# Hybrid decoder layer, down projection: the fourth weight sum of a seven-product unit by an accumulating transfer in place of VectorE

## The chip, the cores and the metric

The kernel runs on one core of one Trainium2 chip. The metric is device time in microseconds; the kernel before takes 2109.56 us (median of three runs, 2108.89 to 2110.98).

## What is computed

One decoder layer over 512 tokens of 2048 features, all in float32: a norm, one input projection, gated linear attention and differential attention side by side, an output projection, and a gated feed-forward part with a causal convolution of width 3. The part that matters here is the last matrix product of it:

```python
def conv_ffn(h, w_ffn_in, conv_w, conv_b, w_ffn_out):
    up = h @ w_ffn_in                                  # 512 x 2048 by 2048 x 11264
    a, b = up[..., :D_FF], up[..., D_FF:]
    ...
    return (jax.nn.gelu(a, approximate=True) * b) @ w_ffn_out   # 512 x 5632 by 5632 x 2048
```

The product with `w_ffn_out` is the down projection. 5120 of its 5632 rows go through the units described next, the other 512 through plain products at the very end.

## The kernel before

**Granules.** A matrix product in float32 is made of three products in a rounded format: the weights and the activations are both split into a high part and a low part, and high by high, high by low and low by high are added in a PSUM bank. Weights come in granules of 128 x 1024 elements (512 KB). For each granule ScalarE copies the raw weights into the high part (L137), VectorE subtracts that from the raw weights to get the low part (L138), and TensorE runs 12 matmuls of 128 x 512 on it (L1348 to L1350; L1348 and L1350 need the high part only, L1349 needs the low part). High and low parts lie in a ring of three places (`ring`), with a spare pair (`xhi`, `xlo`) for some granules. Each engine takes its instructions in a fixed order.

**Units.** The big products are done in blocks of two by two with seven products in place of eight (the Strassen-Winograd scheme). One such unit is an object of class `Unit`. `a` is 4 in the units of the up projection and 2 in those of the down projection (`down_unit`, L1358). There are ten down units, `downs[0]` to `downs[9]`; I call them units 0 to 9. A unit has seven segments of two granules each. They run in the order x0, z0, y0, z1, x1, y1, y2, but the next unit's x0 comes ahead of this unit's y2. Segments x0, z0, y0 and y2 use one running sum of weight blocks, `t`, two tiles in the pool `rt`:

- x0 uses t = B11, loaded by SyncE
- z0 uses t + B12; B12 is added by an accumulating transfer, issued by GpSimd right after x0 has split t (method `more`, L1192 to L1195: `dma_start` with `accum_op=ALU.add`, which reads the block from HBM and adds it to what is in SBUF)
- y0 uses t + B22; B22 is loaded by itself into the pool `raw` and added by VectorE (L1211)
- y2 uses t + B21; B21 is loaded by itself into `raw`, since x1 needs it alone, and added by VectorE (L1229)

Segment z1 uses B22, x1 uses B21, and y1 uses B22 + B12, where B12 is added to B22's tiles by a second pair of accumulating transfers, issued after z1 has split B22. So a unit of the kernel before has two pairs of accumulating transfers, 512 KB each transfer: I call them the x0 pair (needed by z0) and the z1 pair (needed by y1).

**Order.** The work around the change is written in segment order (loop from L1504 on), and a scheduler of the framework places the instructions on each engine; it put each L1229 shortly after the split of its tile in y0, although the text has it after y1. Unit 0 and the first segment of unit 1 are different: they are written out by hand (`run_in_order`, `change_over`, with their own additions at L1412 and their own transfers at L1454).

Of the kernel before, what the change touches and what calls it, by code (L numbers as in the profile page):

```python
# [13 lines left out]
ALU = mybir.AluOpType  # L14
# [21 lines left out]
def hybrid_layer(ctx: ExitStack, tc: tile.TileContext, x, attn_pre_norm, w_in, w_alpha_up, b_alpha,  # L36
# [16 lines left out]
    tt = nc.vector.tensor_tensor  # L53
# [46 lines left out]
    def load(src, a, by=None):  # L100
        raw = wpool.tile([P, GR], F32, name="raw", tag="raw", bufs=4)
        (by or nc.sync).dma_start(out=raw.rearrange("p (a b) -> p a b", a=a), in_=src)
        return raw
# [592 lines left out]
    class InUnit:  # L696
# [21 lines left out]
        def more(self, raws, i, j):  # L718
            for g in range(2):
                nc.gpsimd.dma_start(out=raws[g].rearrange("p (a b) -> p a b", a=4),  # L720
                                    in_=self.block(i, j, g), accum_op=ALU.add)
# [42 lines left out]
        def y0(self):  # L764
            self.b22 = self.load(1, 1)
            for g in range(2):
                tt(self.t[g], self.t[g], self.b22[g], ALU.add)
            self.run("y0", "s2", self.t)
            self.more(self.t, 1, 0)
            self.u10 = block_tile("u10")  # L770
            act(self.u10, self.banks["y"], AF.Copy)
# [13 lines left out]
        def y1(self):  # L785
            self.run("y1", "s7", self.b22)
            tt(self.u11, self.u11, self.banks["y"], ALU.subtract)  # L787
            self.done(1, 1, self.u11)
# [380 lines left out]
    class Unit:  # L1169
# [19 lines left out]
                hl = granule(None, self.a, raws[g], spare=extra[0] and turn[0] % 4 == 0)  # L1189
                self.prods(self.banks[c], op, g, hl, first)  # L1190

        def more(self, raws, j):  # L1192
            for g in range(2):
                nc.gpsimd.dma_start(out=raws[g].rearrange("p (a b) -> p a b", a=self.a),  # L1194
                                    in_=self.block(0, j, g), accum_op=ALU.add)  # L1195

        def x0(self):
            self.t = [load_t(self.block(0, 0, g), self.a) for g in range(2)]
# [9 lines left out]
        def y0(self):  # L1208
            self.b22 = [load(self.block(1, 1, g), self.a) for g in range(2)]
            for g in range(2):  # L1210
                tt(self.t[g], self.t[g], self.b22[g], ALU.add)  # L1211
            self.run("y0", "s2", self.t)
            self.out("y0", self.bank_of("y0"))

        def z1(self):
# [9 lines left out]
        def y1(self):  # L1225
            self.run("y1", "s7", self.b22)
            self.out("y1", self.bank_of("y1"))
            for g in range(2):
                tt(self.t[g], self.t[g], self.b21[g], ALU.add)  # L1229

        def y2(self):
            self.run("y2", "a22", self.t)
# [424 lines left out]
```

## Time and profile before

| What | Before |
|---|---|
| median of the runs | 2109.56 us |
| the profiled execution's own time | 2109.1 us |
| its span, first to last instruction | 2107.4 us |
| granted TensorE clock, mean | 0.995 |
| TensorE busy | 2065.7 us (98%) |
| VectorE busy | 1532.4 us (73%) |
| ScalarE busy | 985.8 us (47%) |
| GpSimd busy | 286.6 us (14%) |
| first and last matmul of the down units (L1348) | 1651.4 and 2054.1 us from the span's start |

Times of single events are counted from the span's start. A timeline row gives start, duration, engine, line, operation, tiles, and in brackets how long the engine sat idle before it and which instruction or transfer ended that. A row of the windows view gives a stretch, its length, the busy time of each engine with its number of instructions, the granted clock, the mean busy share of the 16 DMA engines, and their rate in GB/s. TensorE's matmuls overlap each other by more than a third, so the distance of their starts says more than their durations.

### The profile page before, as it was taken

Reading aid. Unit: us, or ns where it says so; the run is one execution under the profiler, and the core shown is the slowest. Engines: PE = TensorE matmul, PEld = TensorE weight load, DVE = VectorE, ACT = ScalarE, POOL = GpSimd, SP = SyncE. Lnnn points to the kernel's source line nnn. Section 1 sums busy time; section 2 is a strip of 40 time slices with the busy share of each in tenths; the row PEclk is TensorE's granted clock in tenths of the full one; section 3 lists DMA queues with packets and bytes.
Section 4 is the critical chain, followed back from the end, with each engine's and each line's share of the span. In section 5 each row is a group of like instructions: output and inputs, shape, how many; then the busy total and the mean of one; then the engine's idle time right before and its main releaser. Section 6 shows DMA issues by size and latency. Waiting matters only on the chain.

```text
span 2107.4 us, 35508 instructions
## 1 busy us (share of the span) xinstructions
PE 2065.7 (98%) x14449; PEld 1904.8 (90%) x14449; DVE 1532.4 (73%) x1842; ACT 985.8 (47%) x1268; POOL 286.6 (14%) x306
## 2 busy tenths in 40 slices
PE   7999999999999999999999999999999999999997
PEld 6699999999888889899999999999999878887786
DVE  5966777666763255986787877878777878888877
ACT  4544444455563233454554444454454554444443
POOL 0212222222200000011111011110110110111100
PEclk9999999999999999999999999999999999999999
DMA  5388878888755344447667577577676876776763
GB/s 209 102 201 185 200 172 178 179 199 196 172 180 196 99 150 160 138 104 193 151 149 189 144 165 186 133 169 171 157 172 168 231 214 175 186 198 156 172 168 140
DMA packets 280696, 358.60 MB, mean 170 GB/s; under 512 B 14592, under 2 KB 221876, under 8 KB 278612
## 3 DMA queue, kind: packets, MB, share of 16 engines
q1 hardware_dynamic: 191380, 259.85, 36.7%
q0 software_dynamic: 84800, 94.38, 29.8%
q8 instruction: 113, 1.85, 0.4%
q10 hardware_dynamic: 4352, 2.10, 0.3%
q14 instruction: 51, 0.42, 0.1%
HBM read 311.72 MB, written 44.56 MB: 169 GB/s over the span
## 4 chain that ended last, share of the span: by engine, by line
issue 52%; PE 40%; POOL 4%; DMA 2%; DVE 1%; ACT 1%; POOLq 0%; SPq 0%; DVEq 0%; ACTq 0%
PE bank L192 3%; PE bank L193 3%; PE bank L191 3%; PE bank L742 3%; PE bank L744 3%; PE bank L746 3%; PE bank L743 3%; PE bank L747 3%; PE bank L748 3%; POOL rt L1194 2%; POOL raw L1194 2%; PE bank L522 1%; PE bank L1349 1%; PE bank L1350 1%; PE bank L1348 1%
## 5 line engine op out<-in xcount | busy, mean ns | idle before, releaser
L137 ACT ACTIVATE ring<-raw 128x1024 fp32r<-128x1024 f32 x315 | 333.3, 1060 | 518.7 <-PE bank L1247 123.6
L138 DVE TENSOR_TENSOR ring<-raw,ring 128x1024 fp32r<-128x1024 f32 x315 | 384.4, 1224 | 245.5 <-ACT ring L137 242.1
L1248 PE MATMUL bank<-ah,ring 128*128 128x256 f32 x1280 | 353.7, 276 | 0.1
L1246 PE MATMUL bank<-ah,ring 128*128 128x256 f32 x1280 | 353.5, 276 | 0.0
L1247 PE MATMUL bank<-al,ring 128*128 128x256 f32 x1280 | 353.5, 276 | 0.0
L137 ACT ACTIVATE ring<-rt 128x1024 fp32r<-128x1024 f32 x221 | 232.9, 1059 | 232.1 <-PE bank L1247 145.0
L138 DVE TENSOR_TENSOR ring<-rt,ring 128x1024 fp32r<-128x1024 f32 x221 | 269.3, 1222 | 91.9 <-ACT ring L137 90.0
L1248 PEld LDWEIGHTS bank<-ah,ring 128*128 128x128 f32 x1280 | 240.3, 188 | 0.3 <-DVE ring L138 0.3
L1246 PEld LDWEIGHTS bank<-ah,ring 128*128 128x128 f32 x1280 | 240.3, 188 | 0.1
L1247 PEld LDWEIGHTS bank<-al,ring 128*128 128x128 f32 x1280 | 240.3, 188 | 0.1
L1349 PE MATMUL bank<-ring,ah 128*128 128x512 f32 x424 | 166.3, 392 | 6.5 <-DVE ring L138 6.5
L1350 PE MATMUL bank<-ring,al 128*128 128x512 f32 x424 | 165.3, 390 | 0.0
L1348 PE MATMUL bank<-ring,ah 128*128 128x512 f32 x424 | 158.4, 391 | 0.4 <-ACT ring L137 0.4
L191 PE MATMUL bank<-ring,ah 128*128 128x512 f32 x280 | 110.1, 399 | 1.9 <-ACT ring L137 1.9
L192 PE MATMUL bank<-ring,ah 128*128 128x512 f32 x280 | 111.3, 399 | 0.0
L193 PE MATMUL bank<-ring,al 128*128 128x512 f32 x280 | 110.3, 396 | 0.0
L1194 POOL DMA_DIRECT2D raw<-in_w_ffn_in_dram x40 | 51.0, 1277 | 407.3 <-DVE ring L138 404.4
L1349 PEld LDWEIGHTS bank<-ring,ah 128*128 128x128 f32 x424 | 79.6, 188 | 26.6 <-DVE ring L138 10.4
L1348 PEld LDWEIGHTS bank<-ring,ah 128*128 128x128 f32 x424 | 79.5, 188 | 18.9 <-ACT ring L137 2.1
L1350 PEld LDWEIGHTS bank<-ring,al 128*128 128x128 f32 x424 | 79.6, 188 | 16.3
L1194 POOL DMA_DIRECT2D rt<-in_w_ffn_in_dram x40 | 50.9, 1274 | 319.2 <-DVE ring L138 243.1
L746 PE MATMUL bank<-ring,ah 128*128 128x256 f32 x320 | 92.4, 289 | 0.2 <-DVE u L787 0.2
(346 smaller groups left out, 5691.8 us busy)
## 6 DMA issues: line engine op xcount, KB each, us to landing
raw<-in_w_ffn_in_dram SPq DMA_DIRECT2D x96, 512.0 KB, 5.3
raw<-in_w_in_dram SPq DMA_DIRECT2D x56, 512.0 KB, 4.8
raw<-in_w_ffn_out_dram SPq DMA_DIRECT2D x48, 512.0 KB, 6.4
raw<-in_w_in_dram POOLq DMA_DIRECT2D x40, 512.0 KB, 7.1
rt<-in_w_ffn_in_dram SPq DMA_DIRECT2D x40, 512.0 KB, 5.6
rt<-in_w_ffn_in_dram POOLq DMA_DIRECT2D x40, 512.0 KB, 6.1
raw<-in_w_ffn_in_dram POOLq DMA_DIRECT2D x40, 512.0 KB, 7.5
raw<-in_w_o_dram SPq DMA_DIRECT2D x32, 512.0 KB, 4.2
```

The lines of the kernel that those rows point to most:

```text
L137: act(hi, raw, AF.Copy)
L138: tt(lo, raw, hi.bitcast(F32), ALU.subtract)
L191: mm(banks[t], ah[:, t, s, :], w[0][:, k, :], start=st, stop=False)
L192: mm(banks[t], ah[:, t, s, :], w[1][:, k, :], start=False, stop=False)
L193: mm(banks[t], al[:, t, s, :], w[0][:, k, :], start=False, stop=sp)
L1194: nc.gpsimd.dma_start(out=raws[g].rearrange("p (a b) -> p a b", a=self.a), in_=self.block(0, j, g), accum_op=ALU.add)
L1246: mm(o, wh, sh[:, :, kk, :], start=start and kk == 0 and n == 0, stop=False, **NOW)
L1247: mm(o, wh, sl[:, :, kk, :], start=False, stop=False, **NOW)
L1248: mm(o, wl, sh[:, :, kk, :], start=False, stop=kk == HK - 1, **NOW)
L1348: mm(b[j], sh[:, o:o + P], w[0][:, q, :], start=start and st == 0, stop=False, **NOW)
L1349: mm(b[j], sh[:, o:o + P], w[1][:, q, :], start=False, stop=False, **NOW)
L1350: mm(b[j], sl[:, o:o + P], w[0][:, q, :], start=False, stop=st == 3, **NOW)
```

## The change

In down units 1 to 9 VectorE no longer adds B21 to t. In its place, right after y0 has split t, GpSimd issues a pair of accumulating transfers that read B21 from HBM once more and add it to the two tiles of t. I call this the y0 pair. The up projection's units (a == 4) and unit 0 keep VectorE's addition. B21 is still loaded by itself for x1.

```diff
-        def more(self, raws, j):
+        def more(self, raws, j, i=0):
             for g in range(2):
                 nc.gpsimd.dma_start(out=raws[g].rearrange("p (a b) -> p a b", a=self.a),
-                                    in_=self.block(0, j, g), accum_op=ALU.add)
+                                    in_=self.block(i, j, g), accum_op=ALU.add)
...
             self.run("y0", "s2", self.t)
+            if self.a == 2:
+                self.more(self.t, 0, 1)
             self.out("y0", self.bank_of("y0"))
...
         def y1(self):
             self.run("y1", "s7", self.b22)
             self.out("y1", self.bank_of("y1"))
-            for g in range(2):
-                tt(self.t[g], self.t[g], self.b21[g], ALU.add)
+            if self.a == 4:
+                for g in range(2):
+                    tt(self.t[g], self.t[g], self.b21[g], ALU.add)
```

Lines after L1212 have numbers higher by two or three in the changed kernel: L1349 is L1352, L1356 is L1359.

VectorE, from y0 to x1 of unit 4, before. The rows with `rt` at L138 are y0's two splits, those with `raw` are z1's two and the first of x1; L1356 adds a PSUM bank to the output sums, L151 splits activations:

```order
L138 TENSOR_TENSOR ring<-rt,ring 128x1024
L1356 TENSOR_TENSOR acc_16862<-acc_16862,bank 128x512
L1356 TENSOR_TENSOR acc_16863<-acc_16863,bank 128x512
L1229 TENSOR_TENSOR rt<-rt,raw 128x1024
L151 TENSOR_TENSOR al<-st,ah 128x1024
L138 TENSOR_TENSOR ring<-rt,ring 128x1024
L138 TENSOR_TENSOR ring<-raw,ring 128x1024
L1356 TENSOR_TENSOR acc_16862<-acc_16862,bank 128x512
L1229 TENSOR_TENSOR rt<-rt,raw 128x1024
L1356 TENSOR_TENSOR acc_16863<-acc_16863,bank 128x512
L138 TENSOR_TENSOR xlo<-raw,xhi 128x1024
L138 TENSOR_TENSOR ring<-raw,ring 128x1024
```

VectorE at the same place in the changed kernel:

```order
L138 TENSOR_TENSOR ring<-rt,ring 128x1024
L1359 TENSOR_TENSOR acc_16862<-acc_16862,bank 128x512
L1359 TENSOR_TENSOR acc_16863<-acc_16863,bank 128x512
L151 TENSOR_TENSOR al<-st,ah 128x1024
L138 TENSOR_TENSOR ring<-rt,ring 128x1024
L138 TENSOR_TENSOR ring<-raw,ring 128x1024
L1359 TENSOR_TENSOR acc_16862<-acc_16862,bank 128x512
L1359 TENSOR_TENSOR acc_16863<-acc_16863,bank 128x512
L138 TENSOR_TENSOR xlo<-raw,xhi 128x1024
L138 TENSOR_TENSOR ring<-raw,ring 128x1024
```

The two additions are gone, and the rest stands in the same sequence, so y0's second split moves up by one place and z1's second by two.

GpSimd's transfers in the down units, before, from unit 3's z1 pair to unit 5's x0 pair. The names carry buffer numbers: `rt_17950` and `rt_17952` are unit 4's t, `raw_18058` and `raw_18060` its B22:

```order
L1194 DMA raw_17806<-in_w_ffn_out_dram 128x2x512
L1194 DMA raw_17808<-in_w_ffn_out_dram 128x2x512
L1194 DMA rt_17950<-in_w_ffn_out_dram 128x2x512
L1194 DMA rt_17952<-in_w_ffn_out_dram 128x2x512
L1194 DMA raw_18058<-in_w_ffn_out_dram 128x2x512
L1194 DMA raw_18060<-in_w_ffn_out_dram 128x2x512
L1194 DMA rt_18206<-in_w_ffn_out_dram 128x2x512
L1194 DMA rt_18208<-in_w_ffn_out_dram 128x2x512
```

GpSimd's transfers at the same place in the changed kernel, up to unit 5's x0 pair:

```order
L1194 DMA raw_17806<-in_w_ffn_out_dram 128x2x512
L1194 DMA raw_17808<-in_w_ffn_out_dram 128x2x512
L1194 DMA rt_17950<-in_w_ffn_out_dram 128x2x512
L1194 DMA rt_17952<-in_w_ffn_out_dram 128x2x512
L1194 DMA rt_17950<-in_w_ffn_out_dram 128x2x512
L1194 DMA rt_17952<-in_w_ffn_out_dram 128x2x512
L1194 DMA raw_18058<-in_w_ffn_out_dram 128x2x512
L1194 DMA raw_18060<-in_w_ffn_out_dram 128x2x512
L1194 DMA rt_18206<-in_w_ffn_out_dram 128x2x512
L1194 DMA rt_18208<-in_w_ffn_out_dram 128x2x512
```

The y0 pair (the second pair on `rt_17950` and `rt_17952`) stands between unit 4's x0 pair and its z1 pair, so the z1 pair is now behind it on GpSimd and on its queue.

On TensorE the scheduler also changes something: in the kernel before there are 33 places where it put two to four high-part products (L1348) of a granule ahead of the first low-part product (L1349); in the changed kernel there are 15, and elsewhere high, low and third product follow each other matmul by matmul. SyncE's order differs in one place only (two loads swapped in the last 50 us), ScalarE's in one (two neighbours swapped).

## The prediction

> **What bounds the kernel now.** I read the page first, then cut out the stage of the change, then asked there what TensorE waits for.
>
> ```profile
> span 2107.4 us, 35508 instructions
> ...
> q1 hardware_dynamic: 191380, 259.85, 36.7%
> q0 software_dynamic: 84800, 94.38, 29.8%
> ```
>
> The profiled execution took 2109.1 us, 1.7 us more than its span; the median of the runs, 2109.56 us, lies 0.46 us above it. Of the two queue lines keep the prices. All accumulating transfers go by q0. 94.38 MB at 0.524 MB each are 180 transfers, which took 29.8% of 2107.4 us on all 16 engines, so one takes **3.49 us of all 16 DMA engines**. A plain load (q1) of the same size takes 36.7% of 2107.4 us x 0.524 / 259.85 = 1.56 us.
>
> Next, three stretches by windows: the stage from unit 1's y0 to the last down matmul, and two short ones inside it in which one queue alone is at work.
>
> ```profile
> 1711.00:2056.00 345.00, 340.45 (x1490) 278.69 (x1490) 287.73 (x307) 158.12 (x160) 40.18 (x34) 1.00 0.68 176
> 1836.60:1839.00 2.40, 2.40 (x12) 1.99 (x11) 2.40 (x3) 0.00 (x0) 1.19 (x1) 1.00 1.00 170
> 1845.20:1847.00 1.80, 1.80 (x9) 1.49 (x8) 0.25 (x1) 1.34 (x2) 0.00 (x0) 1.00 1.04 399
> ```
>
> In 345 us TensorE is idle for 4.55 us. It bounds the stage, one matmul per 0.23 us (340.45 / 1490), and no change of the other engines can win more than about those **4.55 us**. VectorE is busy for 83% and the DMA engines for 68%. The second row (accumulating transfers alone) has all engines busy at 170 GB/s, the third (plain loads alone) all busy at 399 GB/s: an accumulating transfer really needs more than twice the time, and while it runs nothing else is served for free.
>
> What ends TensorE's idle time in this stage, and the rows of the largest waits:
>
> ```profile
> PE bank L1349 <- DVE ring L138: 3.2, 4, 1.0
> PE bank L1349 <- DVE xlo L138: 1.3, 2, 0.8
> ...
> 1732.83 0.50 PE L1349 MATMUL bank<-ring,ah 128*128 128x512 f32 x1 [0.74 <-DVE ring L138]
> 1832.86 0.50 PE L1349 MATMUL bank<-ring,ah 128*128 128x512 f32 x1 [0.48 <-DVE ring L138]
> 1910.73 0.50 PE L1349 MATMUL bank<-ring,ah 128*128 128x512 f32 x1 [1.03 <-DVE ring L138]
> 1989.81 0.50 PE L1349 MATMUL bank<-ring,ah 128*128 128x512 f32 x1 [0.93 <-DVE ring L138]
> ```
>
> All of it is for a low part from VectorE. But VectorE is the last link only; whether it was late by itself shows in what stood ahead of it. The waits at 1832.86, 1910.73 and 1989.81 are y0's second granule in units 4, 6 and 8, and there it was late by itself:
>
> ```profile
> 1826.99 1.22 DVE L138 TENSOR_TENSOR ring<-rt,ring 128x1024 fp32r<-128x1024 f32 x1
> 1829.32 1.22 DVE L1229 TENSOR_TENSOR rt<-rt,raw 128x1024 f32<-128x1024 f32 x1
> 1830.45 1.22 DVE L151 TENSOR_TENSOR al<-st,ah 128x1024 fp32r<-128x1024 f32 x1
> 1831.59 1.22 DVE L138 TENSOR_TENSOR ring<-rt,ring 128x1024 fp32r<-128x1024 f32 x1
> 1834.24 1.17 POOL L1194 DMA_DIRECT2D raw<-in_w_ffn_out_dram  x1 [19.24 <-DVE ring L138]
> 1837.70 1.19 POOL L1194 DMA_DIRECT2D raw<-in_w_ffn_out_dram  x1 [2.29 <-DVE xlo L138]
> ...
> 1845.66 1.06 ACT L137 ACTIVATE xhi<-raw 128x1024 fp32r<-128x1024 f32 x1 [4.33 <-DMA raw<-in_w_ffn_out_dram]
> 1846.75 1.23 DVE L138 TENSOR_TENSOR xlo<-raw,xhi 128x1024 fp32r<-128x1024 f32 x1 [2.97 <-ACT xhi L137]
> 1849.06 1.06 ACT L137 ACTIVATE ring<-rt 128x1024 fp32r<-128x1024 f32 x1 [0.44 <-PE bank L1350]
> 1849.09 0.39 PE L1349 MATMUL bank<-xlo,ah 128*128 128x512 f32 x1
> ```
>
> This is unit 4. The L1229 at 1829.32 stands between y0's two splits; without it the second split (1831.59) starts 1.13 us sooner. The other half of the fence is the tight place for the change. The z1 pair is issued at 1834.24 and 1837.70; y1's second granule waits for its landing until 1845.66 on an idle ScalarE, is split by 1847.98, and TensorE needs it at 1849.09. The chain has **1.1 us in reserve**. The waits at 1732.83, 1749.99 and 1982.94 (the two with `xlo`) already have such a late landing behind them.
>
> **The change part by part.**
>
> ```profile
> L1229 DVE TENSOR_TENSOR rt<-rt,raw x18: 1218/1222/1226, 1712.4 to 2028.3; 128x1024 f32<-128x1024 f32 x18
> ```
>
> *Removed:* 18 additions, 18 x 1.22 = 22 us of VectorE. On the path are only the three waits above, 0.48 + 1.03 + 0.93 = **2.4 us**; the rest of the 22 us lies beside TensorE's matmuls, and what is late next in those places is y1's second granule.
>
> *Added on GpSimd:* 18 issues of 1.17 us, on an engine busy for 40 of 345 us: nothing by themselves. Each waits for y0's split and then for its turn; behind it stands the z1 pair (order in the section above). Its own reader is y2, split from 1849.06 on, 20 us after y0: covered.
>
> *Added on the DMA engines:* two transfers in each of nine units, 2 x 3.49 = 7.0 us of all engines, ahead of the z1 pair on the same queue. They can begin about 2 us after y0's first split is done (the row of 1826.99 ends at 1828.21; issue 0.3 us later as in the rows of z1, first data about 1.9 us after that, an estimate from the stretch of 1836.60, which the issue at 1834.24 fills). They delay the z1 pair by 7.0 us less what the engines idle from then to the pair's landing. These are the nine stretches, unit 1 to 9, from that start to the end of the data of the pair's second transfer:
>
> ```profile
> 1714.50:1729.90 15.40, 15.40 (x70) 12.75 (x69) 10.97 (x12) 7.63 (x10) 2.36 (x2) 1.00 0.73 172
> 1754.50:1768.20 13.70, 13.70 (x61) 11.07 (x60) 11.85 (x14) 3.18 (x3) 2.36 (x2) 1.00 0.77 168
> 1789.70:1806.10 16.40, 16.40 (x74) 13.60 (x73) 16.16 (x18) 8.82 (x9) 2.36 (x2) 1.00 0.64 143
> 1830.40:1845.20 14.80, 14.31 (x63) 11.56 (x62) 12.90 (x15) 3.19 (x3) 2.36 (x2) 1.00 0.70 155
> 1867.20:1883.70 16.50, 16.50 (x74) 13.68 (x73) 16.26 (x18) 8.81 (x9) 2.36 (x2) 1.00 0.61 147
> 1908.30:1923.00 14.70, 13.67 (x61) 10.96 (x60) 12.86 (x15) 3.18 (x3) 2.36 (x2) 1.00 0.72 151
> 1944.80:1962.90 18.10, 18.10 (x82) 14.98 (x81) 16.24 (x18) 8.78 (x9) 2.36 (x2) 1.00 0.65 162
> 1986.20:2001.90 15.70, 14.77 (x65) 11.91 (x64) 14.05 (x16) 5.22 (x6) 2.39 (x2) 1.00 0.57 104
> 2024.30:2038.90 14.60, 14.60 (x66) 12.09 (x65) 12.85 (x15) 5.75 (x6) 2.36 (x2) 1.00 0.60 111
> ```
>
> Idle is length x (1 - share): 4.2, 3.2, 5.9, 4.4, 6.4, 4.1, 6.3, 6.8, 5.8 us. The delay is 7.0 less that: 2.8, 3.8, 1.1, 2.6, 0.6, 2.9, 0.7, 0.2, 1.2 us. Against it stands the reserve of y1's second granule, read in each unit as above from the end of its split to its first L1349 (unit 1: the row of 1732.83, none; unit 4: 1.1; unit 9 below, 2044.12 - 2041.72 = 2.4).
>
> ```profile
> 2040.49 1.23 DVE L138 TENSOR_TENSOR ring<-raw,ring 128x1024 fp32r<-128x1024 f32 x1 [2.88 <-ACT ring L137]
> ...
> 2044.12 0.39 PE L1349 MATMUL bank<-ring,ah 128*128 128x512 f32 x1
> ```
>
> The reserves are 0.1, 1.1, 2.0, 1.1, 1.3, 1.2, 0.3, 1.3, 2.4 us. What sticks out is new idle time of TensorE: 2.7 + 2.7 + 0 + 1.5 + 0 + 1.7 + 0.4 + 0 + 0 = **9.0 us**. It is counted from TensorE's old position, so the 0.48 and 1.03 us won in units 4 and 6 are swallowed (TensorE only arrives sooner at a granule that is not there); the 0.93 us of unit 8 stays a gain.
>
> *Moved:* TensorE's order becomes high, low, third throughout most granules. Where up to three high products stood ahead, it now asks for the low part up to 3 x 0.23 = 0.7 us sooner. I charge that once, in unit 7, which has no reserve left, and hold it for nothing where y1's reserve stays. The swaps on ScalarE and SyncE cost nothing I can see.
>
> **Sum:** + 9.0 - 0.9 + 0.7 = + 8.8 us on 2109.1, or 2117.9; 0.46 us more for the median: about **2118 us**, 0.4% slower.
>
> The unknown is what a transfer takes that has others ahead and beside it. At 3.1 us (0.524 MB at the 170 GB/s of the second window) the delays shrink by 0.8 each, 9.0 becomes 5.4, and the time 2115. At 1.56 us, the plain load's price, two make 3.1 us, less than the smallest idle time (3.2), and nothing is delayed. On the other side, if only 60% of the idle time can be used, since its pieces come before the second y0 transfer is released or between two others, the overhangs are 4.4, 4.0, 1.5, 3.3, 1.9, 3.3, 2.9, 1.6 and 1.1 us, 24 in all. I take 3.49, the price measured on this queue over all 180, and all of the idle time.
>
> A rule of the Trainium skill gives less than this row. "DMA: Bandwidth & Descriptors", section "Anatomy of one DMA — SWDGE (gpsimd) path", fits a GpSimd transfer as 2.0 us plus its bytes at 436 GB/s: 3.2 us to land for 0.524 MB, of which 1.2 us move data. By that the y0 pair would need 2.4 us of the engines, no z1 pair would be late, and the time would be that of the first rival. No plain GpSimd transfer of this size is in the trace; for accumulating ones it disagrees:
>
> ```profile
> DMA to landing us min/median/max: 5.8/7.8/10.4
> ```
>
> This is L1194 in the stage, with 5.8 us as its best case. I therefore give that rule only the part of the first rival's chance in which the pair's true price is near the lower bound.
>
> **The rivals.**
>
> *It fits into the gaps, and VectorE's relief counts (not slower).* One mechanism, at y0's second granule: the three waits go, and the z1 pair lands within its reserve. It decides where the pair's price falls under idle time plus reserve, 4.3 us in the worst units (3.2 + 1.1 and 4.2 + 0.1), or 2.15 us per transfer. The time is 2109.56 - 2.4 = 2107.2. For it speaks the input projection, which adds its fourth block in this way already:
>
> ```profile
> 320.40:334.20 13.80, 13.80 (x124) 13.80 (x123) 6.64 (x7) 5.22 (x6) 3.79 (x3) 1.00 1.13 180
> ...
> DMA to landing us min/median/max: 6.0/7.1/9.6
> ```
>
> Four accumulating transfers run back to back there (first row; the second is L720's landing) beside a TensorE that never idles. Against it: in that stretch hardly a plain load is in the way (180 GB/s is the rate of accumulating transfers alone), and its units are stretched by attention work between the segments.
>
> *All idle time goes (faster).* If VectorE's relief also brings the transfers' issues forward so far that the late landings heal, 4.55 us go: 2105.0. Against it: VectorE sits idle before y1's granules (2.97 us in the row of 1846.75), so its speed is not what is missing there.
>
> *The queue clogs.* With 60% of the idle time usable: 24 us, 2134. The DMA share would rise from 0.68 by 18 x 3.49 / 345 = 0.18 to 0.86, which leaves little room to make up a delay.
>
> **How the numbers follow.** My forecast (z1 pair late, mostly in units 1, 2, 4 and 6) gets 0.55, the first rival 0.30, clogging 0.08, all idle time gone 0.07. A measurement of this kernel can tell 0.2%, 4.2 us, from no change: under 2105.3 is faster, over 2113.8 slower. The forecast is slower for 0.51 of its 0.55, clogging all of its 0.08; the first rival lies within 0.2% but for 0.03. That gives faster 0.10, same 0.31, slower 0.59. The range goes from 2106, under the first rival, to 2134, the clogging case, and leaves out about 0.15.
>
> **What would show it.** Right: 18 fewer additions and VectorE 22 us less busy; q0 at 198 transfers and about 104 MB; no wait at y0's second granule in units 4, 6 and 8; longer waits of ScalarE for `raw` in y1 and, behind it, of TensorE for y1's second low part, some 1.5 to 3 us in units 1, 2, 4, 6; DMA share in the stage near 0.86. Wrong: z1 pairs that land as before although the y0 pair ran ahead of them; TensorE's new waits at y2 or z0 in place of y1; a y0 transfer that takes well under 3 us of the engines.

## The result, and the profile after

| | before | changed | ratio, 95% interval |
|---|---|---|---|
| median, 12 runs each | 2107.24 us | 2114.44 us | 1.0035 (1.0021 to 1.0048) |
| profiled execution, span | 2109.1, 2107.4 us | 2118.7, 2117.0 us | |

The changed kernel is slower by 0.35%. On the 2109.56 us from which the prediction started, that is 2116.9 us, against 2118 forecast. Beneath that agreement both terms of the sum were too small, as the experiments show.

The page of the changed kernel: the span, the engines, the DMA queues.

```profile
span 2117.0 us, 35547 instructions
...
PE 2066.3 (98%) x14449; PEld 1900.8 (90%) x14449; DVE 1512.8 (71%) x1824; ACT 984.8 (47%) x1268; POOL 308.8 (15%) x324
...
q1 hardware_dynamic: 191380, 259.85, 36.5%
q0 software_dynamic: 89696, 103.82, 32.0%
```

VectorE lost its 18 additions (1842 to 1824), GpSimd gained 18 issues, and q0 moved 103.82 MB, 198 transfers of 0.524 MB: the change does what it says. The queue's time went from 29.8% of 2107.4 to 32.0% of 2117.0 us, so the 18 new transfers took (677.4 - 628.0) / 18 = 2.7 us of all engines each, between the 1.56 and the 3.49 us of the prediction. This is what each added to the queue's time; the same difference gives 2.2 in e2 and 3.0 in e3 below.

Where the time went: the first and last matmul of down granules on a ring tile in both kernels (the line before and its new number after), then the stage by windows in the changed kernel.

```profile
L1348 PE MATMUL bank<-ring,ah x424: 387/389/503, 1651.4 to 2052.7; 128*128 128x512 f32 x142
```

```profile
L1351 PE MATMUL bank<-ring,ah x424: 387/389/505, 1650.4 to 2062.9; 128*128 128x512 f32 x142
```

```profile
1711.00:2066.00 355.00, 343.70 (x1484) 276.64 (x1483) 265.96 (x287) 155.84 (x160) 61.75 (x52) 1.00 0.81 197
```

The stage of the down products is 412.5 us long after and 401.3 before: 11.2 us more, against 9.6 more in the profiled executions. TensorE idles 11.3 of 355 us in it (4.55 of 345 before). The DMA share rose from 0.68 to 0.81, not to 0.86.

What ends TensorE's idle time in that window of the changed kernel (columns: waiting line and releaser, us in total, times, longest):

```profile
PE bank L1352 <- DVE xlo L138: 5.8, 9, 0.9
PE bank L1352 <- DVE ring L138: 3.4, 5, 0.8
PE bank L1351 <- ACT xhi L137: 1.3, 3, 0.4
PE bank L1351 <- ACT ring L137: 0.9, 2, 0.5
```

Six waits became nineteen, and some are now for ScalarE's high part. VectorE is again only the last link. Unit 4 in the order of time, as in the prediction's fence:

```profile
1831.04 1.22 DVE L138 TENSOR_TENSOR ring<-rt,ring 128x1024 fp32r<-128x1024 f32 x1
1832.56 1.17 POOL L1194 DMA_DIRECT2D rt<-in_w_ffn_out_dram  x1 [14.01 <-DVE ring L138]
1834.51 1.22 DVE L138 TENSOR_TENSOR ring<-rt,ring 128x1024 fp32r<-128x1024 f32 x1
1836.02 1.19 POOL L1194 DMA_DIRECT2D rt<-in_w_ffn_out_dram  x1 [2.29 <-DVE ring L138]
1837.16 1.26 POOL L1194 DMA_DIRECT2D raw<-in_w_ffn_out_dram  x1
1837.97 1.22 DVE L138 TENSOR_TENSOR xlo<-raw,xhi 128x1024 fp32r<-128x1024 f32 x1
1839.49 1.19 POOL L1194 DMA_DIRECT2D raw<-in_w_ffn_out_dram  x1 [1.07 <-DMA st<-sd3s]
...
1850.47 1.06 ACT L137 ACTIVATE xhi<-raw 128x1024 fp32r<-128x1024 f32 x1 [3.00 <-DMA raw<-in_w_ffn_out_dram]
1851.56 1.23 DVE L138 TENSOR_TENSOR xlo<-raw,xhi 128x1024 fp32r<-128x1024 f32 x1 [1.64 <-ACT xhi L137]
1852.84 0.50 PE L1352 MATMUL bank<-xlo,ah 128*128 128x512 f32 x1 [0.66 <-DVE xlo L138]
```

The y0 pair (`rt`) is issued at 1832.56 and 1836.02, the z1 pair (`raw`) at 1837.16 and 1839.49. The last of it lands at 1850.47, 11.0 us after its issue (8.0 before: 1837.70 to 1845.66). The split ends at 1852.79, TensorE stands there, and the 1.1 us of reserve are gone. Over the nine units the landing of the z1 pairs, 18 transfers, before and after:

```profile
DMA to landing us min/median/max: 5.8/7.7/10.4
```

```profile
DMA to landing us min/median/max: 8.7/10.4/15.1
```

### The profile page after: what moved, and what is told of

It is laid out like the page before. It is cut to its first block, busy times and chain, and to the rows that moved or that the text cites. A ratio compares the mean times of both kernels' runs of the same rounds, so it can differ in the third digit from the quotient of the medians.

```text
span 2117.0 us, 35547 instructions
## 1 busy us (share of the span) xinstructions
PE 2066.3 (98%) x14449; PEld 1900.8 (90%) x14449; DVE 1512.8 (71%) x1824; ACT 984.8 (47%) x1268; POOL 308.8 (15%) x324
## 3 DMA queue, kind: packets, MB, share of 16 engines
q0 software_dynamic: 89696, 103.82, 32.0%
## 4 chain that ended last, share of the span: by engine, by line
PE 51%; issue 34%; DMA 6%; DVE 3%; POOL 3%; ACT 2%; POOLq 0%; SPq 0%; ACTq 0%; DVEq 0%
PE bank L1250 6%; PE bank L1251 6%; PE bank L1249 6%; DMA rt<-in_w_ffn_out_dram 3%; PE bank L192 3%; PE bank L193 3%; PE bank L742 3%; PE bank L191 3%; PE bank L744 3%; PE bank L743 3%; PE bank L746 3%; PE bank L748 3%; PE bank L747 3%; POOL rt L1194 1%; POOL raw L1194 1%
## 5 line engine op out<-in xcount | busy, mean ns | idle before, releaser
L138 DVE TENSOR_TENSOR ring<-raw,ring 128x1024 fp32r<-128x1024 f32 x315 | 384.1, 1222 | 272.2 <-ACT ring L137 271.4
L138 DVE TENSOR_TENSOR ring<-rt,ring 128x1024 fp32r<-128x1024 f32 x221 | 269.1, 1221 | 87.6 <-ACT ring L137 87.4
L1352 PE MATMUL bank<-ring,ah 128*128 128x512 f32 x424 | 166.8, 393 | 6.7 <-DVE ring L138 6.7
L1352 PEld LDWEIGHTS bank<-ring,ah 128*128 128x128 f32 x424 | 79.5, 188 | 27.8 <-DVE ring L138 11.7
```

The costliest lines, as they stand in the source:

```text
L138: tt(lo, raw, hi.bitcast(F32), ALU.subtract)
L1352: mm(b[j], sh[:, o:o + P], w[1][:, q, :], start=False, stop=False, **NOW)
```

## The experiments

Each kernel was timed in five rounds beside the kernel before, on one chip per group (e1 to e4, e5 to e8, e9 to e11, e12); ratios are to the kernel before of the same group. For a common measure I took from each trace the starts of successive matmuls. An undisturbed one follows after 0.227 us; what goes beyond that (where the step is over 0.26 us) is charged to the granule of the later matmul. Between y1 and y2 of unit 9 TensorE runs twelve products of the closing part (L1552 to L1554 before, from 2046.62 to 2049.11); they are work and count as such, and what is lost at them is charged to y2. Sums in us over units 1 to 9, from one profiled execution each (unit 1's x0 and z0 left out, as they lie ahead of the change; y1 holds both granules, z0, x0 and y2 likewise):

| kernel | ratio (95%) | y0, 2nd | y1 | z0 | x0 | y2 | all |
|---|---|---|---|---|---|---|---|
| before | 1 | 3.5 | 1.3 | 2.3 | 0 | 0.1 | 7.2 |
| changed | 1.0035 (1.0021-1.0048) | 0.5 | 10.7 | 5.0 | 1.9 | 0.2 | 18.2 |
| e1 no add | 0.9963 (0.9949-0.9976) | 0 | 0 | 0.6 | 0 | 0 | 0.6 |
| e2 behind z1 | 1.0033 (1.0022-1.0044) | 0.1 | 0.4 | 2.2 | 0 | 11.6 | 14.4 |
| e3 first tile | 0.9980 (0.9968-0.9992) | 0.2 | 0.8 | 1.1 | 1.7 | 0 | 4.4 |
| e4 plain copy | 0.9983 (0.9969-0.9997) | 0.5 | 0.5 | 2.3 | 1.4 | 0 | 4.7 |
| e5 add itself | 1.0002 (0.9992-1.0012) | 3.9 | 3.1 | 2.6 | 0 | 0.8 | 10.4 |
| e6 not unit 7 | 1.0019 (1.0006-1.0032) | 0.2 | 0.6 | 3.6 | 0 | 9.3 | 13.7 |
| e7 GpSimd adds | 1.0107 (1.0089-1.0125) | 9.1 | 18.3 | 3.5 | 0.4 | 0.6 | 32.8 |
| e8 first behind z1 | 0.9979 (0.9968-0.9990) | 0.3 | 0 | 0 | 0 | 1.2 | 1.5 |
| e9 adds later | 0.9967 (0.9956-0.9979) | 0 | 0 | 0 | 0 | 1.3 | 1.3 |
| e10 second behind z1 | 0.9967 (0.9956-0.9979) | 1.6 | 0.1 | 1.0 | 0 | 0 | 2.7 |
| e11 not 7 and 9 | 0.9987 (0.9978-0.9995) | 0.3 | 1.4 | 3.5 | 0 | 0.1 | 5.3 |
| e12 later, not 9 | 0.9959 (0.9942-0.9975) | 0 | 0 | 0 | 0 | 1.2 | 1.2 |

(z1 lost 0.6 us in e3 and 1.0 in e7, nothing elsewhere.) One profiled execution and the median of the runs differ by a few us, and two profiles of one schedule do too (before and e5: 7.2 and 10.4); the ratios are the verdicts, the columns say where. The expectations of e6, e11 and e12 were written with the time of the closing products, 2.7 us, still counted as lost in unit 9.

The diffs of e1 to e4 are against the changed kernel, that of e6 against e2, the others against the kernel before.

**e1: neither add nor transfer.**

```diff
             self.run("y0", "s2", self.t)
-            if self.a == 2:
-                self.more(self.t, 0, 1)
```

> In units 1 to 9 the block B21 is neither added by VectorE nor transferred into the running sum: the fourth sum is left out, so y2's product is of another matrix. TensorE's instructions stand in the same order as in the changed kernel. Theory T1 (the y0 pair's engine time ahead of the z1 pair on the queue makes y1's second granule late): all new stalls go and y0's second granule stays on time, so about 3 us less than before, ratio 0.9985 (0.998 to 0.9995). Rival T2 (TensorE's new order, low products asked for sooner, costs by itself): the loss stays, ratio 1.001 to 1.004. Rival T3 (two more issues on GpSimd's queue) and rival T4 (the DMA engines as a whole are short of time) expect what T1 expects here.

Measured: 2098.98 us, before 2108.28. TensorE's instructions stand as in the changed kernel, so the order (T2) costs nothing by itself: that rival is out. But the gain is 7.8 us by the ratio (5.1 to 10.7), not 3. All of TensorE's waits in the stage in e1, and then the same 337 us of the kernel before and of e1 by windows:

```profile
PE bank L1350 <- DVE xlo L138: 0.3, 1, 0.3
```

```profile
1711.00:2048.00 337.00, 332.45 (x1455) 272.05 (x1455) 284.02 (x304) 156.11 (x158) 40.18 (x34) 1.00 0.68 177
```

```profile
1711.00:2048.00 337.00, 336.70 (x1486) 278.46 (x1485) 270.72 (x288) 160.02 (x159) 40.19 (x34) 1.00 0.68 180
```

Before, 1455 matmuls start in that time, in e1 1486: 31 more at 0.227 us (336.70 / 1486), 7.0 us (6.6 by the table's columns). The idle column had shown 4.55 us only, since after these waits the first matmul takes 0.50 us and counts as busy. By e1 the transfers alone, without VectorE's relief, cost 1.0035 - 0.9963 = 0.0072, 15 us (11 to 19 by the two intervals).

**e2: the y0 pair behind the z1 pair.**

```diff
         def z1(self):
             self.run("z1", "s3", self.b22)
             self.more(self.b22, 1)
+            if self.a == 2:
+                self.more(self.t, 0, 1)
```

(The two lines are gone from y0, and GpSimd is held to this order.)

> The y0 pair's two accumulating transfers are issued behind the z1 pair instead of ahead of it; everything else as in the changed kernel. T1: the z1 pair's second transfer lands again about 8 us after its issue (10 to 12 in the changed kernel), y1's second granule loses 1 to 2 us in nine units instead of 8.0, y0's second granule 0.5; ratio 0.9985 to 1.000. T4: the same engine time only pushes other transfers; the x0 pair or the plain loads become late instead, z0's granules lose 8 us or more, ratio 1.002 to 1.005. T2 (matmul order, which stays but for two places): 1.003.

Measured: 2115.16 us, before 2108.28. T1 is right on its place: y1 loses 0.4 us in place of 10.7. T4 is right on the sum: the time is lost elsewhere, though not at z0. Most of it, 9.2 us, is one place, y2 of unit 7 (the rest is at unit 9), shown here by windows, SyncE's issue, ScalarE's split and TensorE's wait:

```profile
1950.00:1975.00 25.00, 20.64 (x90) 16.44 (x88) 14.79 (x17) 8.25 (x9) 5.98 (x5) 1.00 1.07 271
```

```profile
1958.19 0.34 SPq L48 DMA_DIRECT2D st<-ud  x1
...
1973.11 1.06 ACT L150 ACTIVATE ah<-st 128x1024 fp32r<-128x1024 f32 x1 [9.14 <-DMA st<-ud]
...
1976.17 0.76 PE L1353 MATMUL bank<-ring,ah 128*128 128x512 f32 x1 [5.50 <-ACT ah L150]
```

For 25 us the DMA engines have no free time (share 1.07). A load of SyncE's queue issued at 1958.19 lands 15 us later, and ScalarE waits 9.14 us for it with the split of the granule that TensorE needs behind it. Behind this wait there is a second loss:

```profile
1976.00:1982.00 6.00, 5.55 (x12) 4.08 (x13) 6.00 (x8) 3.02 (x4) 0.00 (x0) 0.50 0.53 144
```

For these 6 us the granted clock was 0.50 (1.00 in the stage before the wait), and 12 matmuls started where some 26 would have. So a late landing of this length cost TensorE the wait and some us at half the clock.

**e3: only the first tile by a transfer.** Method `more` takes the tiles as an argument here.

```diff
-                self.more(self.t, 0, 1)
+                self.more(self.t, 0, 1, (0,))
...
-            if self.a == 4:
-                for g in range(2):
+            for g in range(2) if self.a == 4 else (1,):
                     tt(self.t[g], self.t[g], self.b21[g], ALU.add)
```

> Only the first of the two tiles of the running sum gets B21 by a transfer; the second is still added by VectorE. T1: one transfer takes 3.5 us of the engines, and they idle 3.2 to 6.8 us ahead of the z1 pair's landing in every unit, so hardly anything is pushed; the add that stood between y0's two splits is gone all the same. y1's second granule loses about 2 us in nine units, y0's 0.5 to 1; ratio 0.9985 to 1.000. T4 (engine time as such): half of the changed kernel's loss, ratio 1.0015 to 1.002. T3 (a second kind of transfer in the queue at all): as the changed kernel, 1.003.

Measured: 2102.51 us, before 2108.28, faster by 4.2 us. Half the transfers do not cost half of the change's loss: they cost less than the relief wins. By the columns, one transfer per unit mostly fits into the engines' idle time (y1 loses 0.8 us, x0 1.7). T3 and T4 in its plain form fall here.

**e4: a plain copy at the same place.**

```diff
-                self.more(self.t, 0, 1)
+                for g in range(2):
+                    nc.gpsimd.dma_start(out=self.t[g].rearrange("p (a b) -> p a b", a=self.a), in_=self.block(1, 0, g))
```

> The y0 pair is issued at the same place on the same queue with the same bytes, but copies B21 over the running sum instead of adding it, so y2's product is of B21 alone. TensorE's order is that of the changed kernel. T1 in terms of engine time: if a plain copy on this queue takes 1.6 us of the engines as SyncE's plain loads do, the pair needs 3.1 us, fits into the idle time, and the ratio is 0.9985 to 1.000; its landing is 4 us or less, against 5.8 and more for the accumulating one. T3 (the two issues and the place in the queue cost, not the engine time): 1.003, as the changed kernel.

Measured: 2104.25 us, before 2108.28. Its queue line, and the landing of the 18 copies:

```profile
q0 software_dynamic: 87392, 103.82, 31.0%
```

```profile
DMA to landing us min/median/max: 4.0/4.4/7.0
```

The same bytes, the same place on the queue and the same TensorE order as in the changed kernel, and it is faster than before. By the queue's share a copy takes (0.310 x 2104.0 - 628.0) / 18 = 1.35 us of all engines (the rounding of the shares leaves 0.1), half of an accumulating one. So the place in the queue is not the cost; what the accumulation takes is. A copy is shorter on the engines and lands sooner, and this run doesn't separate the two; e2, where a load of another queue was late at a DMA share of 1.07, speaks for the engines. The two copies are not free either: by the medians e4 is some 4 us above e1, with intervals that overlap.

On the copy, the Trainium skill's page "DMA: Bandwidth & Descriptors", section "Anatomy of one DMA — SWDGE (gpsimd) path", gives by its fit an estimate of 3.2 us for 0.524 MB; the best of 18 took 4.0. For the accumulating transfers, at best 5.8 us, it is too low by more. The fit makes no difference between the two kinds; here the measurement does.

**e5: VectorE adds as before, but not B21.**

```diff
-                tt(self.t[g], self.t[g], self.b21[g], ALU.add)
+                tt(self.t[g], self.t[g], self.b21[g] if self.a == 4 else self.t[g], ALU.add)
```

> The kernel before, with one operand changed: in units 1 to 9 VectorE adds the running sum to itself instead of B21 to it (the fourth sum is another one, so y2's product is too). Every instruction of every engine stands at its old place and the add takes the same time, but B21's tile is free for the next load once x1 is split. This tells apart what the removal of the add was worth in e1 (7.8 us less than before). Theory V (VectorE's time, 22 us): ratio 1.000 (0.9988 to 1.0012). Theory B (the B21 tile is given back earlier, so loads come earlier): as e1, 0.996 to 0.998.

Measured: 2107.12 us, before 2106.81, no difference. The traces show why: in all nine units of the kernel before, both adds run ahead of x1's splits of B21 (unit 4: 1829.32 and 1834.45, x1's first split at 1837.32). The add never was the tile's last reader, so the edit gives nothing back earlier, and theory B falls by that order rather than by the time. What is left for the gain of e1 is VectorE's add, its time or its place, and the matmul order that came with its removal; e8 to e10 take these up.

**e6: as e2, without unit 7.**

```diff
-            if self.a == 2:
+            if self.a == 2 and self is not downs[7]:
                 self.more(self.t, 0, 1)
```

> As e2 (y0 pair behind the z1 pair), but unit 7 keeps VectorE's adds and has no y0 pair. In e2 TensorE lost 8.6 us at one place in unit 7, where a load for ScalarE's split landed 15 us after its issue while all DMA engines were taken for 25 us, and 2.5 us more in unit 9. Theory T1 with that place as an accident of unit 7: both go, ratio 0.998 to 0.9995. T4 (the stage has no room for the engine time anywhere; take it away here and it comes out elsewhere): 1.001 to 1.003.

Measured: 2111.29 us, before 2106.81. The long wait in unit 7 is gone, but at y2 of unit 9 8.5 us are lost now. GpSimd's issues, ScalarE's wait and TensorE's there:

```profile
2025.61 1.19 POOL L1194 DMA_DIRECT2D raw<-in_w_ffn_out_dram  x1 [1.15 <-DVE ring L138]
2026.34 2.89 POOL L1194 DMA_DIRECT2D rt<-in_w_ffn_out_dram  x2
...
2044.41 1.06 ACT L137 ACTIVATE xhi<-rt 128x1024 fp32r<-128x1024 f32 x1 [5.92 <-DMA rt<-in_w_ffn_out_dram]
2046.46 0.82 PE L1557 MATMUL bank<-ring,ah 128*128 128x512 f32 x2 [4.52 <-ACT ring L137]
```

In unit 9 no x0 stands between y1 and y2, so the y0 pair, now last on the queue, is itself the late one. TensorE waits for a closing product (L1557), whose split stands behind that of the late tile on ScalarE. My miss: I had read e2's loss in unit 9 as an echo of unit 7.

**e7: GpSimd adds.**

```diff
-                tt(self.t[g], self.t[g], self.b21[g], ALU.add)
+                if self.a == 4:
+                    tt(self.t[g], self.t[g], self.b21[g], ALU.add)
+                else:
+                    nc.gpsimd.tensor_tensor(out=self.t[g], in0=self.t[g], in1=self.b21[g], op=ALU.add)
```

> The fourth sum is added by GpSimd itself (18 adds of 128x1024 in units 1 to 9), neither by VectorE nor by a transfer; TensorE's order is that of the changed kernel. GpSimd is busy for some 40 of 345 us in this stage, but its adds stand ahead of the z1 pair's issue. Its price is in no trace of this case yet. If an add takes no more than 3 us, it ends before the z1 pair can be issued: ratio 0.996 to 0.998, near e1. If it takes over 5 us, or if VectorE's own instructions get longer beside it, z1 pair and splits come late: 1.000 to 1.005.

Measured: 2129.43 us, before 2106.81, the slowest of all. GpSimd's adds (count, least, median and longest in ns), then unit 5 on GpSimd and VectorE:

```profile
L1232 POOL TENSOR_TENSOR rt<-rt,raw x18: 2382/3318/3453, 1708.2 to 2045.6; 128x1024 f32<-128x1024 f32 x18
```

```profile
1870.98 0.68 DVE L1359 TENSOR_TENSOR acc<-acc,bank 128x512 f32<-128x512 f32 x1
1871.15 2.39 POOL L1232 TENSOR_TENSOR rt<-rt,raw 128x1024 f32<-128x1024 f32 x1 [12.08 <-DVE ring L138]
...
1876.98 1.22 DVE L138 TENSOR_TENSOR ring<-raw,ring 128x1024 fp32r<-128x1024 f32 x1
1877.14 3.33 POOL L1232 TENSOR_TENSOR rt<-rt,raw 128x1024 f32<-128x1024 f32 x1 [3.60 <-DVE xlo L138]
1880.42 1.17 POOL L1194 DMA_DIRECT2D raw<-in_w_ffn_out_dram  x1
...
1879.31 2.24 DVE L151 TENSOR_TENSOR al<-st,ah 128x1024 fp32r<-128x1024 f32 x1
```

VectorE's add takes 1.22 us. Of GpSimd's, seven take 2.4 us, and each of them begins while VectorE adds a PSUM bank (the row at 1870.98); eleven take 3.3 to 3.45, and each of them begins while a split of VectorE runs for another 1.1 us (the row at 1876.98). The z1 pair is issued only behind the adds. VectorE's own split, 1.22 us elsewhere, takes 2.24 beside an add (at most 3.4 in this stage), and in the fence it ends 1.1 us after the add. That agrees with the Trainium skill, "SBUF — State Buffer", section "🔬 SBUF: two separate sides", by which a VectorE operation with two inputs in SBUF and a GpSimd operation that reads SBUF take turns at a shared port for a whole instruction. I had expected near e1 for an add around 3 us, and for longer instructions of VectorE 1.005 at most; the loss is twice that.

**e8: the first tile by a transfer, behind the z1 pair.** The edit is e3's, with the transfer at e2's place.

> As e3 (only the first tile's B21 by a transfer, the second by VectorE), with the transfer issued behind the z1 pair instead of ahead of it. T1: y1's second granule loses nothing more (0.8 us in nine units in e3), ratio 0.997 to 0.998. T4: the x0 pair and the loads beside it lose what y1 gains, ratio as e3, 0.998, or above, to 1.000.

Measured: 2101.48 us, before 2106.81. y1 and z0 lose nothing, but the ratio is e3's within the intervals, so the time doesn't tell T1 from T4.

**e9: VectorE keeps all adds, later, and nothing is transferred.**

```diff
-                tt(self.t[g], self.t[g], self.b21[g], ALU.add)
+                if self.a == 4:
+                    tt(self.t[g], self.t[g], self.b21[g], ALU.add)
+                else:
+                    tc.keep_in_program_order(nc.vector.tensor_tensor(out=self.t[g], in0=self.t[g], in1=self.b21[g], op=ALU.add))
```

> The kernel before without any new transfer: VectorE keeps all 18 adds of B21, but they are held behind y1's second split on its instruction stream instead of standing between y0's splits and behind them. The matmul order changes in places and some loads change their order on SyncE. Theory P (what the removal was worth is the place of the first add, between y0's two splits): ratio 0.997 to 0.999. Theory V (VectorE's 22 us as such): 0.9995 to 1.0015, since none of it is saved; above that if the two adds in a row make y2's or the next x0's splits late.

Measured: 2099.91 us, before 2107.24, faster by 7.0 us with all of VectorE's work in place. Theory V falls. Unit 4 on VectorE and GpSimd, z1's first split, y0's two, z1's second, and the z1 pair:

```profile
1817.86 1.23 DVE L138 TENSOR_TENSOR ring<-raw,ring 128x1024 fp32r<-128x1024 f32 x1 [0.20 <-ACT ring L137]
1819.39 1.17 POOL L1194 DMA_DIRECT2D raw<-in_w_ffn_out_dram  x1 [14.45 <-DVE ring L138]
1819.60 1.22 DVE L138 TENSOR_TENSOR ring<-rt,ring 128x1024 fp32r<-128x1024 f32 x1
1823.07 1.22 DVE L138 TENSOR_TENSOR ring<-rt,ring 128x1024 fp32r<-128x1024 f32 x1
1824.81 1.22 DVE L138 TENSOR_TENSOR xlo<-raw,xhi 128x1024 fp32r<-128x1024 f32 x1
1826.32 1.19 POOL L1194 DMA_DIRECT2D raw<-in_w_ffn_out_dram  x1 [5.76 <-DVE xlo L138]
...
1833.26 1.06 ACT L137 ACTIVATE xhi<-raw 128x1024 fp32r<-128x1024 f32 x1 [2.05 <-DMA raw<-in_w_ffn_out_dram]
1834.35 1.23 DVE L138 TENSOR_TENSOR xlo<-raw,xhi 128x1024 fp32r<-128x1024 f32 x1 [0.57 <-ACT xhi L137]
...
1840.82 0.39 PE L1352 MATMUL bank<-xlo,ah 128*128 128x512 f32 x1
```

The second z1 transfer is issued at 1826.32, and y1's second granule is ready at 1835.58, 5.2 us before TensorE asks for it (1.1 us before). That issue waits for z1's second split. Before, this split stood behind both adds, the one at 1829.32 of the prediction's fence and this one:

```profile
1834.45 1.22 DVE L1229 TENSOR_TENSOR rt<-rt,raw 128x1024 f32<-128x1024 f32 x1
...
1836.19 1.22 DVE L138 TENSOR_TENSOR xlo<-raw,xhi 128x1024 fp32r<-128x1024 f32 x1
```

The scheduler moved more than the adds in e9. In unit 4 z1's first split is now ahead of y0's on VectorE (the row at 1817.86; 1832.72, behind both, before), the loads have another order, and TensorE has 59 places with several high products first, where the kernel before has 33. So e9 shows that VectorE's 22 us need not go; how much of the 7.0 us is the adds' place it doesn't show. The matmul order is no common cause of the gains, though: e1 and e10 gain as much with 15 such places.

**e10: the second tile by a transfer, behind the z1 pair.** The mirror of e8: the second tile by a transfer, the first one's add stays with VectorE. ScalarE's order is that of the kernel before.

> The mirror of e8: behind the z1 pair one transfer adds B21 to the second tile, and VectorE keeps the first tile's add, the one that stands between y0's two splits. Same engine time for the DMA engines and for VectorE as e8 (ratio 0.998). Theory P (place): y0's second granule loses its 3 us again, ratio 0.9993 to 1.001. Theory V (VectorE's time): as e8, 0.997 to 0.9985.

Measured: 2101.10 us, before 2107.24. Theory P in its narrow form (only the add between y0's splits counts) falls too: that add is still there, at 1828.42 in unit 4,

```profile
1826.08 1.22 DVE L138 TENSOR_TENSOR ring<-rt,ring 128x1024 fp32r<-128x1024 f32 x1
1828.42 1.21 DVE L1233 TENSOR_TENSOR rt<-rt,raw 128x1024 f32<-128x1024 f32 x1
...
1830.69 1.22 DVE L138 TENSOR_TENSOR ring<-rt,ring 128x1024 fp32r<-128x1024 f32 x1
...
1834.15 1.21 DVE L138 TENSOR_TENSOR xlo<-raw,xhi 128x1024 fp32r<-128x1024 f32 x1
```

and the gain is e8's or more; y0 loses 1.6 us in place of 3.5. But from y0's second split to z1's second it is 3.46 us here and 4.60 before (1831.59 to the 1836.19 above), one add less. Both adds stood in VectorE's order ahead of z1's second split, in all nine units; either one out, or both later, lets the z1 pair start sooner. Counted from y0's first matmul in unit 4, its second transfer is issued after 8.7 us before, 8.0 in e8, 6.7 in e10, 4.8 in e9 and 4.0 in e1. That reading fits e8, e9 and e10 together; no run tested it alone.

**e11: as e6, without unit 9.** The edit is e6's with `downs[9]` excepted as well.

> As e6 (y0 pair behind the z1 pair, unit 7 by VectorE), but unit 9 keeps VectorE's adds as well. In e6 TensorE lost 11.3 us ahead of y2's first granule of unit 9, 8.5 more than before, where the y0 pair landed 17 us after its issue beside the last group's loads. T1 with two crowded places (units 7 and 9): that goes too, ratio 0.997 to 0.9995. T4 (no room for the engine time anywhere): 1.001 to 1.003.

Measured: 2103.27 us, before 2107.24. With the two crowded places spared, the pair behind z1 is faster than the kernel before, and T4 as a law of the whole stage falls: it holds in units 7 and 9. Some cost of the 14 transfers is left: e1, which also drops the adds of those two units, is another 5 us faster.

**e12: as e9, with unit 9 as before.** The edit is e9's for units 1 to 8 alone.

> As e9 (no new transfer, VectorE's adds held behind y1's second split), but in unit 9 the adds stay where they were before: there y2 follows y1 directly, and in e9 y2's first granule of unit 9 lost 6.8 us, 4.1 more than before. If the late adds are the cause of that, those 4.1 us come back and everything else stays: ratio 0.994 to 0.996. If they aren't (the last group's loads and splits are), 0.9965 as e9.

Measured: 2101.30 us, before 2109.56. In the profile y2 of unit 9 loses nothing again. But there was less to win than expected: in e9 TensorE ran 24 closing products ahead of the rest of y2, not 12, so of the 6.8 us named above 5.4 were work and 1.4 were lost, and e12 loses 1.2 us at y2 of unit 1 instead. The intervals of e9 and e12 overlap, so the times don't tell them apart. With e10 they are the fastest versions of the full computation by their medians: 7 to 9 us under the kernel before, some 15 under the changed one; e9 and e12 need no new transfer for it.

## Why the prediction was right, and where it was not

Right in sign, size and place of the main loss: z1 pairs late, y1 waiting. That the size came out is in part luck. By its steps:

- **y1's overhang, + 9.0.** The losses at y1 grew from 1.3 to 10.7 us, + 9.4. By units 1 to 9 they grew by 2.5, 1.4, 0.2, 0.9, 1.3, 1.9, 0.7, 0.5 and 0 us, where the sum had 2.7, 2.7, 0, 1.5, 0, 1.7, 0.4, 0, 0: the total fits, the units only roughly. The sum was for y1's second granule alone, and that one grew by 6.7. The other 2.7 us are y1's first granule, 1.8 of them in unit 1, where it had 0.8 us in reserve; the sum left it out. A transfer added less engine time than charged (2.7 us, not 3.49), so less of the idle time must have been of use; that is worked out backwards and no run shows it.
- **VectorE's relief, - 0.9.** This is the step that failed: "no change of the other engines can win more than about those 4.55 us", and of those only 0.93 kept. e1 wins 7.8 us. The waits at y0 were worth 3.5 us by matmul starts, not 2.4, and 3.0 of them are gone in the changed kernel; whether a part came back as waiting at y1, as the sum has it for units 4 and 6, the columns don't tell. And the bound of 4.55 us counted idle time only, where 31 matmuls, 7.0 us, were missing.
- **The argument against the rival "all idle time goes"**, that VectorE waits for ScalarE ahead of y1 and so its speed is not what is missing, fell with e1 and e10. VectorE was late some 10 us earlier, at z1's split, which releases the z1 pair. By the reading under e10, the late landing for which VectorE then sat idle was in part its own doing.
- **What the transfers cost.** By the difference to e1 15 us, not 9.7. Beside y1, z0 and x0 lost 4.6 us that the sum did not hold: plain loads and the x0 pair behind the same engines (argued from the DMA share of 0.81; no run took it apart).
- **Matmul order, + 0.7.** Nothing in e1, which has that order.
- **"It fits into the gaps"** was right for one transfer per unit (e3) and, nearly, for two plain copies (e4). For the accumulating pair the condition, under 2.15 us each, was not met at 2.7.
- **Its signs.** The waits at y0 went but for 0.5 us, and y1 waits longer, but its second granule lost 0.9 to 1.6 us in units 1, 2, 4 and 6, not 1.5 to 3. Two signs of being wrong showed beside the right ones: new losses at z0, and a transfer that adds under 3 us.

The net came out near because a relief that was too small by some 7 us stood against a cost that was too small by some 5. This is luck: neither of the two terms was right.

## What to carry to other kernels

An instruction off the critical path can still hold a queue that releases a transfer: follow the late landing back to the issue and what released the issue, before calling the engine's idle time ahead of it proof of spare speed. Try moving the work within its engine's order before moving it to another engine: here that, with what the scheduler moved along with it, gave as much as the best-placed transfer, at no DMA time. And take the bound on what can be won from the count of instructions that start in a window, not from the idle column.

## What the runs showed of the hardware

- An accumulating transfer of 0.524 MB from GpSimd's queue took 3.5 us of all 16 DMA engines in the mean over the kernel before, further ones added 2.2 to 3.0 us each, and it landed after 5.8 us at best; a plain copy from the same queue added 1.35 us and landed after 4.0 at best.
- With the DMA share at 1.07 for 25 us, a load of SyncE's queue took 15 us to land beside accumulating transfers of GpSimd's.
- After waits of up to 1.1 us in the down stage of the kernels before and changed, TensorE's first matmul took 0.50 us in the records (0.39 otherwise), so a wait cost more than its idle time. After waits of 5.50 us (e2) and 4.52 us (e6) the granted clock was 0.50 for some 7 us, and matmuls started every 0.43 us in place of 0.227.
- A GpSimd add of 128x1024 took 2.4 us where it began beside VectorE's addition of a PSUM bank and 3.3 to 3.45 where it began beside a split; VectorE's splits beside it took up to 3.4 us in place of 1.22, its additions of a PSUM bank 0.68 as ever.
